# Three steps of an attention loop, each cut in two, with the second half at a later position

## The chip, the cores and the metric

The kernel runs on one core of a Trainium2 chip. A core has a matrix engine (PE in the profile, with its weight loads as PEld), a vector engine (DVE), a scalar engine (ACT), a general engine (POOL) and a queue engine that issues most transfers (SP). Each engine executes its own list of instructions in order, and waits for the others by semaphores. The metric is the device time of one launch in microseconds (us); of the kernel before, three runs are shown.

## The reference

One inference step of a trunk with two layers on 384 tokens (256 latent ones and 128 context ones, computed together, `NT` = 384). A layer is: half a SwiGLU feed-forward, a mixer, half a feed-forward, each behind an RMS norm whose scale, shift and gate come from a conditioning vector through a large weight (`w_ada`, 1024 x 9216). The mixer has three branches on one input projection:

```
q, k, v (6 heads, two key halves of 32)        differential attention, then
  o = rms_norm(o, subln_w) * (1 - lam_init)
cq -> rms_norm -> @ w_q_up (256 x 576)         6 heads of 96; the last 32 of each get rotary
ckv -> rms_norm -> keys and values             MLA softmax attention
u -> S5 scans -> y = gelu(y); y * sigmoid(y @ w_glu + b_glu)
out = concat(o_a, o_b, o_c) @ w_out
```

All of it is float32. The big products are made of three rounded products each (high by high, high by low, low by high).

## The kernel before, in words

Activations lie transposed (channels on the 128 partitions, tokens along the row). Most of the time goes to the two feed-forwards of each layer (`up`, `down`). The change is in the mixer's attention loop, which runs once in each layer, at about 425 to 575 us and 1250 to 1372 us of the profiled execution.

The loop has 36 units (`ORDER`): 18 of differential attention (`DA`, 'd') and 18 of MLA ('m'). A unit is one query tile `t` of one head or half: `scores` makes the products (`sc`; for DA four at once, each on 32 partitions), the maximum (`nm`, DVE), the exponential with its sum (`e`, ACT) and the scaling; three positions later (`LOOK`) `finish` transposes the weights (`wtp`) and, for the last tile, multiplies by the values (`po`). Other work is hung on the loop's positions by `put(i, step)`; what stands at position `i` is written `LEAD` = 2 units ahead of unit `i`. `AT` holds the positions of the steps that prepare MLA:

- `mla_q(t)`, for three token tiles: four products (`pq`), two copies on ACT into `qt2`, the rotation on DVE for the first two tiles, then six transposes (`qt2p`) and two copies into `qT2`. Its weight (`in_wsm`) takes one of the three `raw` buffers until the last tile is done.
- `norm_stats` and `norm_apply`, in the loop as `da_stats(b)` and `da_apply(b)`, for each of three head pairs once its `po` is done: squares on ACT (`nsq`), three small products (`npr<-co,nsq`), 13 tiny DVE instructions for the reciprocal root, six products that spread it (`npr<-co,tiny`), one DVE product, and the split for the output projection. Both steps stand at the same position.
- `s5_y` at the first position: gelu on ACT (`yg`), eight transposes (`ytp`), copies. `glu` follows at position 5.

Between them, `fill` issues pieces of the `w_ada` product for later layers: a load of 1 MB into a `raw` buffer (`in_wada`) and products `adaps`, four at once, each into 32 of the array's columns. All products write into a pool of seven PSUM banks. The order in which each engine gets its instructions isn't the order of the code: when the program is built, a scheduler plays it against a model of the engines and puts down at each time what is ready. So a change of one step moves the rows of others near it, and outside the loops nothing.

Of the kernel before, what the change touches and what calls it, by code (L numbers as in the profile page):

```python
# [9 lines left out]
F32 = mybir.dt.float32  # L10
FR = mybir.dt.float32r
I32 = mybir.dt.int32
AF = mybir.ActivationFunctionType
# [11 lines left out]
ORDER = 'd'*12+'dmm'*6+'m'*6  # L25
PF = (3, 8)
PFN = 1
LEAD, LOOK, QLEAD, DELAY, LAG, KCV = 2, 3, 4, 3, 0, 1
F0, F1 = 0, 36
AT = (0, 1, 2, 2, 3, 4, 4, 4, 5, 5, 7, 8, 8, 10, 11, 12, 13, 14)  # L30
AT5 = (0, 5)
YB = 8
KO = (6, 7, 0, 1, 2, 3, 4, 5)
# [143 lines left out]
def trunk(ctx, tc, I, O):  # L177
# [8 lines left out]
    def bank(name):  # L186
        return psp.tile([128, 512], F32, tag="P", name=name)
# [15 lines left out]
    hsum = co[:, CO['hsum'][0]:CO['hsum'][1]]  # L203
# [8 lines left out]
    def tt(out, a, b, op, eng=None):  # L212
        return (eng or V).tensor_tensor(out, a, b, op=op)  # L213

    def mul(out, a, b, eng=None):
        return tt(out, a, b, ALU.mult, eng)

    def add(out, a, b, eng=None):
        return tt(out, a, b, ALU.add, eng)
# [13 lines left out]
    def act(out, a, f, **k):  # L233
        S.activation(out, a, f, **k)  # L234
# [564 lines left out]
    def mixer(l, h, norm, P, s5stack, after, gate):  # L799
        oh, ol = [None], [None]  # L800
        with ExitStack() as ctx2:
            mp = ctx2.enter_context(tc.tile_pool(name="mix", bufs=1, reuse_waits="tile"))
# [30 lines left out]
            def scaled(ps, p=slice(0, 128), f=None):  # L833
                bb = mp.tile([128, 2], F32, tag="bb", name="bb", bufs=3)
                t = t384("pjt")
                if f is None:
                    V.tensor_copy(bb[p], ps[p, NT:NT + 2])
                    mul(t[p], ps[p, :NT], st['R'][p])
                else:
                    ts(bb[p], ps[p, NT:NT + 2], f)  # L840
                    stt(t[p], ps[p, :NT], f, st['R'][p], ALU.mult, ALU.mult)
                return t, bb

            def t384(name):
                return mp.tile([128, 384], F32, tag="t384", name=name, bufs=YB)
# [14 lines left out]
            def evac(ps):  # L860
                t, bb = scaled(ps)
                for c, lo_, hi_ in CR:
                    biased(t[:, lo_:hi_], t, bb, c)
                return t
# [25 lines left out]
            for z, ps in enumerate(p0):  # L890
                t, bb = scaled(ps)
                for c, lo_, hi_ in CR:
                    biased(uT[:, z, lo_:hi_], t, bb, c)
            vv = mp.tile([96, 8, 8, 16], F32, tag="vv", name="vv")
# [77 lines left out]
                    if nz is not None:  # L972
                        V.memset(fr[:, :, :, nz], 0.0)

            def norm_stats(tiles, sums, e=None):
                ps = [bank("npr") for _ in tiles]
                pm, c = ps[0][:, NT:512], 0
                for grp, sv in zip(tiles, sums):
                    n = sv.shape[-1]
                    sqs = []  # L980
                    for t in grp:
                        sqs.append(t384("nsq"))
                        act(sqs[-1], t, AF.Square)
                    for i in range(3):
                        for j, sq in enumerate(sqs):
                            T.matmul(pm[:, c + n * i:c + n * i + n], sq[:, 128 * i:128 * i + 128], sv,
                                     start=(j == 0), stop=(j == len(grp) - 1))
                    c += 3 * n
                return tiles, ps, rsqrt_small(pm[:, :c], c, e)
# [59 lines left out]
            v2, t = evac(p5[0]), evac(p5[1])  # L1049
# [23 lines left out]
            ap = ctx2.enter_context(tc.tile_pool(name="att", bufs=1, side="right", reuse_waits="tile"))  # L1073

            yT = mp.tile([128, 2, NT], F32, tag="t768", name="yT", bufs=4)

            def s5_y():
                yg = mp.tile([128, 8, 8, 16], F32, tag="vv", name="yg")
                for a in range(2):
                    act(yg.rearrange("p t g c -> p g t c")[:, 4 * a:4 * a + 4],  # L1080
                        py[a].rearrange("p (g t c) -> p g t c", g=4, t=8), AF.Gelu_apprx_tanh)
                for hf in range(2):
                    pt = bank("ytp")
                    for t in range(4):
                        T.transpose(pt[:, t * 128:(t + 1) * 128], yg[:, 4 * hf + t].rearrange("p g c -> p (g c)"),
                                    ident)
                    src = pt.rearrange("p (t g n) -> p g n t", t=4, g=2)[:, :, 0:48, :]
                    for g2 in range(2):
                        V.tensor_copy(yT[:, g2].rearrange("p (n t) -> p n t", t=8)[:, :, 4 * hf:4 * hf + 4], src[:, g2])
# [11 lines left out]
            def out_block(b, src):  # L1101
                act(oh[0][b][:, :NT], src, AF.Copy)
                sub(ol[0][b][:, :NT], src, oh[0][b][:, :NT])
# [36 lines left out]
            def rope(dst, src, nh, t):  # L1140
                a = t384("rsa").rearrange("p (h e) -> p h e", e=32)[:, 0:nh]
                b = t384("rsb").rearrange("p (h e) -> p h e", e=32)[:, 0:nh]
                mul(a, src, cosT[:, t, None, :].broadcast_to([128, nh, 32]))
                for x in range(2):
                    sv = src[:, :, 16 * x:16 * x + 16].rearrange("p n (h e) -> p n h e", h=2)
                    mul(b[:, :, 16 * x:16 * x + 16].rearrange("p n (h e) -> p n h e", h=2), sv[:, :, ::-1, :],
                        sinT[:, t, 16 * x:16 * x + 16].rearrange("p (h e) -> p h e", h=2)[:, None]
                        .broadcast_to([128, nh, 2, 8]))
                add(dst, a, b)
# [12 lines left out]
            su0 = [ap.tile([128, 6], F32, tag="su0", name="su0", bufs=3) for _ in range(3)]  # L1162
# [22 lines left out]
            oT = qT  # L1185
# [2 lines left out]
            ts(sw, SMV('subln')[:, l:l + 1], 1.0 - (0.8 - 0.6 * math.exp(-0.3 * l)))  # L1188
            dst = {}

            def da_stats(b):
                mul(su0[b], su0[b], su0[b])
                dst[b] = norm_stats([[oT[:, b]]], [hsum], su0[b])

            def da_apply(b):
                norm_apply(dst[b], [[sw]], [[[((0, NT), oT[:, b])]]])
                out_block(b, oT[:, b])
# [73 lines left out]

            wqb = []

            def mla_q(t):
                if not wqb:
                    wqb.append(load(I['wsm'][l, :, 0:1152], 1152)[:, :1152].rearrange("p (k n) -> p k n", k=2))
                wq = wqb[0]
                qt2 = ap.tile([128, 576], F32, tag="qt", name="qt2", bufs=2)
                for z in range(2):
                    pq = bank("pq")  # L1280
                    for k in range(2):
                        T.matmul(pq[:, 0:288], cT[:, k, t * 128:(t + 1) * 128], wq[:, k, 288 * z:288 * z + 288],
                                 start=(k == 0), stop=(k == 1))
                    act(qt2[:, 288 * z:288 * z + 288], pq[:, 0:288], AF.Copy)
                if t < 2:
                    pev = qt2.rearrange("p (h e) -> p h e", e=96)[:, :, 64:96]
                    rope(pev, pev, 6, t)
                for z in range(2):
                    pt = bank("qt2p")
                    for h_ in range(3):  # L1290
                        T.transpose(pt[:96, h_ * 128:(h_ + 1) * 128], qt2[:, (3 * z + h_) * 96:(3 * z + h_) * 96 + 96],
                                    ident)
                    act(qT2[:, 3 * z:3 * z + 3, t * 128:(t + 1) * 128],
                        pt[:96, :NT].rearrange("p (h n) -> p h n", h=3), AF.Copy, scale=MLA_SCALE)

            def mla_v(t):
                pt = bank("vt2p")
                T.matmul(pt[:, :384], ckT[:, t * 128:(t + 1) * 128], wv, start=True, stop=True)
                S.copy(vt2[:, t], pt[:, :384])
# [15 lines left out]
                units.append((da if c == 'd' else mla).pop(0))  # L1315
            KC = V.tensor_copy if KCV else S.copy
            pre = {}
            early = ([lambda t=t: mla_q(t) for t in range(3)] + [lambda t=t: mla_v(t) for t in range(4)])
            wraw = {}

            def wo(m, k0, k1, eng=None):
# [12 lines left out]
            def put(i, *fs):  # L1334
                pre.setdefault(i, []).extend(fs)

            def run(n, u, z, h):
                return lambda: late.__setitem__(n, part(u, z, h))

            prep = [lambda: None, lambda: None, lambda: cq_out(0), run('p6', 6, 1, 0), run('p6', 6, 1, 1),  # L1340
                    run('p7', 7, 0, 0), lambda: cq_out(1), lat_stats, run('p7', 7, 0, 1), kpe, lat_norm] + early
            for i, f in zip(AT, prep):
                put(i, f)
            put(AT5[0], s5_y)
            put(AT5[1], glu)
            for i, (kind, b, h2, t, wt) in enumerate(units):
                if t == 0 and h2 == 0 and kind == 'mla':
                    pre.setdefault(i, []).append(lambda b=b: mla_keys(b))
            for i, (kind, b, h2, t, wt) in enumerate(units):
                if kind == 'da' and h2 == 1 and t == 2:  # L1350
                    put(i + LOOK + LEAD + DELAY, lambda b=b: da_stats(b))
                    put(i + LOOK + LEAD + DELAY + LAG, lambda b=b: da_apply(b))
            for m in range(8):
                put(LEAD + W0 + W1 * m // 8, lambda m=m: wo(m, 0, NK1, G if WP else None))
            nfill = len(fillers)
# [1 line left out]
            for i in range(-LEAD, max(len(units) + LOOK, max(pre) - LEAD + 1)):  # L1357
                for f in pre.get(i + LEAD, []):
                    f()
                if 0 <= i < len(units):  # L1360
                    kind, b, h2, t, wt = units[i]
# [169 lines left out]
```

## Time and profile before

| | |
|---|---|
| runs shown | 1693.69 us (median of three), 1690.03 to 1694.74 |
| profiled execution | 1691.62 us, of which the span from first to last instruction is 1689.1 us |
| PE busy | 1638.3 us, 97% of the span |
| DVE, ACT, POOL busy | 65%, 41%, 9% |
| PE's share of the chain that ended last | 87% |
| granted clock of PE, mean | 0.992 of full speed |

PE is the engine that sets the time: the others wait for it. Its "busy" is an upper bound, since the end of a product is modelled. A list of PE in order of time gives the start of each run of like products, how long until the last is done, and in brackets the idle time before it and what ended it. Products overlap, so the cost of a run is best read from its start to the start of the next one. Each float32 product stands as two records in such a list (a transpose as one): "x8" of `sc` or `adaps` are four products.

### The profile page before, as it was taken

To read this page: it belongs to the slowest core of one execution; us is meant where nothing else is said; L and a number is where in the kernel's file an instruction comes from. 1 tells how busy PE (TensorE), PEld (TensorE's weight loads), DVE (VectorE), ACT (ScalarE), POOL (GpSimd) and SP (SyncE) were. 2 spreads that over 40 slices of the span, in tenths; PEclk is the share of its full clock that TensorE was granted. 3 is DMA by queue.
4 is the path that set the end of the run, shared out by engine and by line. 5 is a ranking of instruction groups with operands and counts; after the bars stand their busy time and mean duration, and the time that the engine had idled before them with its cause. 6 is when DMAs were issued, how large, how long until landed. Compare 5 with 4: busy or idle time off the path is not lost.

```text
span 1689.1 us, 26142 instructions
## 1 busy us (share of the span) xinstructions
PE 1638.3 (97%) x10144; PEld 1491.4 (88%) x10144; DVE 1099.7 (65%) x2752; ACT 690.1 (41%) x1295; POOL 157.5 (9%) x220
## 2 busy tenths in 40 slices
PE   7999999999999999999999999999998899999997
PEld 6888999998545889999999999999974589999997
DVE  5974577758456788577575555557655766555555
ACT  4332333433455543333343333334345654333333
POOL 1220010023001400000000000001311140000000
PEclk9999999999999999999999999999999999999998
DMA  9564543443477443353344333435337133333432
GB/s 376 194 222 154 146 148 105 145 175 117 154 275 276 159 140 135 125 137 120 100 152 173 119 126 112 143 94 172 133 113 251 51 116 114 124 121 118 138 97 84
DMA packets 45931, 251.47 MB, mean 149 GB/s; under 512 B 5600, under 2 KB 10576, under 8 KB 23920
## 3 DMA queue, kind: packets, MB, share of 16 engines
q1 hardware_dynamic: 41360, 241.12, 41.4%
q0 software_dynamic: 2144, 4.54, 1.1%
q10 hardware_dynamic: 2304, 4.15, 0.8%
q8 instruction: 79, 1.29, 0.3%
q14 instruction: 44, 0.36, 0.1%
HBM read 246.73 MB, written 3.05 MB: 148 GB/s over the span
## 4 chain that ended last, share of the span: by engine, by line
PE 87%; DVE 6%; ACT 3%; DMA 2%; issue 2%; POOL 0%; ACTq 0%; SPq 0%; DVEq 0%; POOLq 0%
PE up L239 15%; PE up L241 14%; PE up L240 14%; PE down L239 7%; PE down L241 7%; PE down L240 7%; PE adaps L293 4%; PE pj L239 2%; PE pj L241 2%; PE pj L240 2%; DMA raw<-in_wada 1%; PE pout L241 1%; PE pout L239 1%; PE pout L240 1%; PE po L1174 1%
## 5 line engine op out<-in xcount | busy, mean ns | idle before, releaser
L234 ACT ACTIVATE whi<-raw 128x1024 fp32r<-128x1024 f32 (+3 forms) x360 | 332.5, 926 | 658.8 <-PE up L240 333.5
L239 PE MATMUL up<-hh,whi 128*128 128x386 f32 x1408 | 474.4, 342 | 7.8 <-ACT whi L234 4.0
L241 PE MATMUL up<-hh,wlo 128*128 128x386 f32 x1408 | 478.5, 340 | 0.6 <-DVE wlo L213 0.6
L240 PE MATMUL up<-hl,whi 128*128 128x386 f32 x1408 | 478.5, 340 | 0.0
L213 DVE TENSOR_TENSOR wlo<-raw,whi 128x1024 fp32r<-128x1024 f32 (+2 forms) x318 | 347.7, 1093 | 49.3 <-ACT whi L234 46.5
L239 PEld LDWEIGHTS up<-hh,whi 128*128 128x128 f32 x1408 | 266.2, 190 | 15.6 <-ACT whi L234 5.3
L241 PEld LDWEIGHTS up<-hh,wlo 128*128 128x128 f32 x1408 | 265.7, 189 | 9.0 <-DVE wlo L213 2.2
L240 PEld LDWEIGHTS up<-hl,whi 128*128 128x128 f32 x1408 | 266.3, 189 | 1.6 <-issue 1.1
L241 PE MATMUL down<-hidh,wlo 128*128 128x384 f32 x704 | 236.3, 336 | 0.0
L239 PE MATMUL down<-hidh,whi 128*128 128x384 f32 x704 | 235.8, 335 | 0.0
L240 PE MATMUL down<-hidl,whi 128*128 128x384 f32 x704 | 235.3, 334 | 0.0
L231 DVE SCALAR_TENSOR_TENSOR xTt<-down,gate,xTt 128x256 f32<-128x256 f32 (+1 forms) x256 | 95.1, 414 | 114.9 <-PE down L241 114.9
L466 DVE COPY bb<-up 128x2 f32<-128x2 f32 x176 | 27.8, 159 | 190.0 <-PE up L241 189.5
L241 PEld LDWEIGHTS down<-hidh,wlo 128*128 128x128 f32 x704 | 132.1, 188 | 1.1 <-issue 0.6
L239 PEld LDWEIGHTS down<-hidh,whi 128*128 128x128 f32 x704 | 132.2, 188 | 1.0 <-ACT whi L234 0.8
L240 PEld LDWEIGHTS down<-hidl,whi 128*128 128x128 f32 x704 | 132.2, 188 | 0.0
L213 DVE TENSOR_TENSOR t<-up,R 128x384 f32<-128x384 f32 x176 | 95.5, 549 | 3.3 <-ACT R L234 3.2
L293 PE MATMUL adaps<-raw,conds 128*32 128x256 f32 (+1 forms) x704 | 84.7, 498 | 3.6 <-DMA raw<-in_wada 3.6
L239 PE MATMUL pj<-hh,whi 128*128 128x386 f32 (+1 forms) x240 | 83.2, 348 | 0.9 <-ACT whi L234 0.7
L234 ACT ACTIVATE hidh<-sl 128x384 fp32r<-128x384 f32 x88 | 46.1, 524 | 91.1 <-DVE sl L231 91.1
L241 PE MATMUL pj<-hh,wlo 128*128 128x386 f32 (+1 forms) x240 | 82.1, 343 | 1.2 <-DVE wlo L213 1.2
L240 PE MATMUL pj<-hl,whi 128*128 128x386 f32 (+1 forms) x240 | 81.5, 341 | 0.0
(268 smaller groups left out, 1953.0 us busy)
## 6 DMA issues: line engine op xcount, KB each, us to landing
raw<-in_wfi SPq DMA_DIRECT2D x85, 1024.0 KB, 4.9
raw<-in_wada SPq DMA_DIRECT2D x64, 1024.0 KB, 5.7
raw<-in_wfo SPq DMA_DIRECT2D x32, 768.0 KB, 4.2
raw<-in_wfo SPq DMA_DIRECT2D x32, 640.0 KB, 3.9
raw<-in_win SPq DMA_DIRECT2D x14, 1024.0 KB, 4.8
araw<-in_wada SPq DMA_DIRECT2D x8, 1024.0 KB, 9.8
raw<-in_wout SPq DMA_DIRECT2D x16, 512.0 KB, 3.5
wr<-in_wfi SPq DMA_DIRECT2D x8, 384.0 KB, 9.7
```

Source lines behind the costliest of these rows:

```text
L213: return (eng or V).tensor_tensor(out, a, b, op=op)
L231: return V.scalar_tensor_tensor(out, a, s, b, op0=op0, op1=op1)
L234: S.activation(out, a, f, **k)
L239: T.matmul(out, whi, xhi, start=first, stop=False)
L240: T.matmul(out, whi, xlo, start=False, stop=False)
L241: marks.append(T.matmul(out, wlo, xhi, start=False, stop=last).ins)
L293: T.matmul(ps[32 * q:32 * q + 32, 0:w], conds[:, k, :], raw[:, c0:c0 + w], start=(k == 0), stop=(k == 7))
L466: V.tensor_copy(bb[:, z], ps[z][:, NT:NT + 2])
L1174: T.matmul(po[64 * h2:64 * h2 + 64, 0:256], vt[:, kt, 128 * b + 64 * h2:128 * b + 64 * h2 + 64], wTs[h2][:, kt, :], start=(kt == 0), stop= ...
```

## The change

Each of the three steps is cut where PE has to wait for what ACT and DVE make of its products. `mla_q(t)` ends after the rotation, and the transposes are a step of their own, `mla_qt(t)`, two positions later (8 and 10, 9 and 11, 10 and 12; before, the first two tiles were at 8 and the third at 10). The tile `qt` gets a third buffer for it. The differential norm has its squares at position `i+6` of a head pair's last unit `i`, the sums and the root at `i+7`, the spreading at `i+9`; before, all of it was at `i+8`. The gelu stays at position 0, and its transposes come at 2. The instructions are the same in kind and number on each engine.

```diff
-LEAD, LOOK, QLEAD, DELAY, LAG, KCV = 2, 3, 4, 3, 0, 1
+LEAD, LOOK, QLEAD, KCV = 2, 3, 4, 1
-AT = (0, 1, 2, 2, 3, 4, 4, 4, 5, 5, 7, 8, 8, 10, 11, 12, 13, 14)
+AT = (0, 1, 2, 2, 3, 4, 4, 4, 5, 5, 7, 8, 10, 9, 11, 10, 12, 11, 12, 13, 14)
...
+            def norm_squares(tiles):
+                sqs = []
+                for grp in tiles:
+                    sqs.append([t384("nsq") for t in grp])
+                    for sq, t in zip(sqs[-1], grp):
+                        act(sq, t, AF.Square)
+                return sqs
...
-            def norm_stats(tiles, sums, e=None):
+            def norm_stats(tiles, sums, e=None, squares=None):
                 ps = [bank("npr") for _ in tiles]
                 pm, c = ps[0][:, NT:512], 0
-                for grp, sv in zip(tiles, sums):
+                for grp, sv, sqs in zip(tiles, sums, squares or norm_squares(tiles)):
                     n = sv.shape[-1]
-                    sqs = []
-                    for t in grp:
-                        sqs.append(t384("nsq"))
-                        act(sqs[-1], t, AF.Square)
...
-            def s5_y():
-                yg = mp.tile([128, 8, 8, 16], F32, tag="vv", name="yg")
+            yg = mp.tile([128, 8, 8, 16], F32, tag="vv", name="yg")
+
+            def s5_gelu():
                 for a in range(2):
                     act(yg.rearrange("p t g c -> p g t c")[:, 4 * a:4 * a + 4],
                         py[a].rearrange("p (g t c) -> p g t c", g=4, t=8), AF.Gelu_apprx_tanh)
+
+            def s5_y():
...
+            def da_squares(b):
+                mul(su0[b], su0[b], su0[b])
+                dst[b] = norm_squares([[oT[:, b]]])
+
             def da_stats(b):
-                mul(su0[b], su0[b], su0[b])
-                dst[b] = norm_stats([[oT[:, b]]], [hsum], su0[b])
+                dst[b] = norm_stats([[oT[:, b]]], [hsum], su0[b], dst[b])
...
-                qt2 = ap.tile([128, 576], F32, tag="qt", name="qt2", bufs=2)
+                qt2 = qts[t] = ap.tile([128, 576], F32, tag="qt", name="qt2", bufs=3)
...
                 if t < 2:
                     pev = qt2.rearrange("p (h e) -> p h e", e=96)[:, :, 64:96]
                     rope(pev, pev, 6, t)
+
+            def mla_qt(t):
+                qt2 = qts[t]
                 for z in range(2):
                     pt = bank("qt2p")
...
-            early = ([lambda t=t: mla_q(t) for t in range(3)] + [lambda t=t: mla_v(t) for t in range(4)])
+            early = [f for t in range(3) for f in (lambda t=t: mla_q(t), lambda t=t: mla_qt(t))]
+            early += [lambda t=t: mla_v(t) for t in range(4)]
...
-            put(AT5[0], s5_y)
+            put(AT5[0], s5_gelu)
+            put(AT5[0] + 2, s5_y)
...
-                    put(i + LOOK + LEAD + DELAY, lambda b=b: da_stats(b))
-                    put(i + LOOK + LEAD + DELAY + LAG, lambda b=b: da_apply(b))
+                    put(i + LOOK + LEAD + 1, lambda b=b: da_squares(b))
+                    put(i + LOOK + LEAD + 2, lambda b=b: da_stats(b))
+                    put(i + LOOK + LEAD + 4, lambda b=b: da_apply(b))
```

SP's list, which issues the loads, is the same row for row, and in each layer's loop POOL has one copy of a key moved by one place against a split. The lists of PE, ACT and DVE change within the two loops alone. Three places of PE's list in the second layer follow; the line numbers of the changed kernel are a little higher. `pq` and `qt2p` are the query projection and its transposes, `sc` scores, `adaps` the `w_ada` product, `wtp` transposed weights, `po` the product with the values, `npr` the norm, and `vt2p` MLA's values.

PE before, from the first query projection on:

```order
L1282 MATMUL pq<-raw,cT 128x288 x2
L293 MATMUL adaps<-raw,conds 32x512 x4
L1282 MATMUL pq<-raw,cT 128x288 x2
L293 MATMUL adaps<-raw,conds 32x512 x4
L1291 MATMUL qt2p<-co,qt_12963 96x128 x6
L1282 MATMUL pq<-raw,cT 128x288 x4
L293 MATMUL adaps<-raw,conds 32x512 x4
L1291 MATMUL qt2p<-co,qt_12988 96x128 x6
L1212 MATMUL sc<-kT,qT 128x384 x4
L1167 MATMUL wtp<-co,e 128x128 x3
L293 MATMUL adaps<-raw,conds 32x512 x4
```

PE now, from the same place:

```order
L1294 MATMUL pq<-raw,cT 128x288 x2
L1222 MATMUL sc<-kT,qT 128x384 x3
L1294 MATMUL pq<-raw,cT 128x288 x2
L1222 MATMUL sc<-kT,qT 128x384
L1174 MATMUL wtp<-co,e 128x128 x3
L293 MATMUL adaps<-raw,conds 32x512 x4
L1294 MATMUL pq<-raw,cT 128x288 x2
L293 MATMUL adaps<-raw,conds 32x512 x4
L1294 MATMUL pq<-raw,cT 128x288 x2
L1174 MATMUL wtp<-co,e 128x128
L1306 MATMUL qt2p<-co,qt_12963 96x128 x6
L1294 MATMUL pq<-raw,cT 128x288 x4
```

The transposes of the first tile stood behind its products and one run of `adaps`; now one score product, four transposed weights, two runs of `adaps` and the whole second tile's projection lie between. The four scores that stood together are three and one.

PE before, from the third tile on:

```order
L1167 MATMUL wtp<-co,e 128x128
L1282 MATMUL pq<-raw,cT 128x288 x4
L1291 MATMUL qt2p<-co,qt_13061 96x128 x6
L1212 MATMUL sc<-kT,qT 128x384 x4
L1167 MATMUL wtp<-co,e 128x128
L293 MATMUL adaps<-raw,conds 32x256 x8
L1174 MATMUL po<-wT,vtm 64x256 x6
L1177 MATMUL po<-wTp,vtm 64x128
L1298 MATMUL vt2p<-wsm,ckT 128x384
```

PE now, from the third tile's projection:

```order
L1294 MATMUL pq<-raw,cT 128x288 x4
L1222 MATMUL sc<-kT,qT 128x384
L293 MATMUL adaps<-raw,conds 32x512
L1222 MATMUL sc<-kT,qT 128x384
L293 MATMUL adaps<-raw,conds 32x512 x3
L1222 MATMUL sc<-kT,qT 128x384 x2
L1174 MATMUL wtp<-co,e 128x128
L1181 MATMUL po<-wT,vtm 64x256 x6
L1184 MATMUL po<-wTp,vtm 64x128
L1306 MATMUL qt2p<-co,qt_13007 96x128 x6
L1313 MATMUL vt2p<-wsm,ckT 128x384
```

The third tile's transposes, which came straight behind its products, aren't among these rows any more (they come after the next `adaps`); those of the second tile stand among them. The scores of one unit stand in three pieces, with one `adaps` product and then the other three between them.

PE before, around the first head pair's norm:

```order
L1237 MATMUL pk<-ckT,wsm 128x512
L293 MATMUL adaps<-raw,conds 32x256 x8
L986 MATMUL npr<-co,nsq 128x2 x3
L1167 MATMUL wtp<-co,e 128x128 x3
L1298 MATMUL vt2p<-wsm,ckT 128x384
L1212 MATMUL sc<-kT,qT 128x384 x4
L293 MATMUL adaps<-raw,conds 32x256 x8
L1167 MATMUL wtp<-co,e 128x128 x3
L1252 MATMUL sc<-kTh,qT_12625 128x384
L1167 MATMUL wtp<-co,e 128x128
L999 MATMUL npr<-co,tiny 64x128 x6
```

PE now, from the last `adaps` run ahead of that norm:

```order
L293 MATMUL adaps<-raw,conds 32x256 x5
L990 MATMUL npr<-co,nsq 128x2 x3
L1222 MATMUL sc<-kT,qT 128x128 x4
L1174 MATMUL wtp<-co,e 128x128 x3
L1313 MATMUL vt2p<-wsm,ckT 128x384
L293 MATMUL adaps<-raw,conds 32x256 x8
L1247 MATMUL pk<-ckT,wsm 128x512
L1174 MATMUL wtp<-co,e 128x128 x3
L1313 MATMUL vt2p<-wsm,ckT 128x384
L1222 MATMUL sc<-kT,qT 128x384 x3
L1003 MATMUL npr<-co,tiny 64x128 x6
L293 MATMUL adaps<-raw,conds 32x256 x3
```

The squares' sums (`npr<-co,nsq`) keep their place between `adaps` and `wtp`. A run of eight `adaps` products ahead of them is cut in three and five by `vt2p`, and the next unit's scores have moved in behind them.

## Rows read from the trace of the kernel before

**Rows 1.** The page: PE's busy time, and the issues of `in_wada` loads

```profile
PE 1638.3 (97%) x10144; PEld 1491.4 (88%) x10144; DVE 1099.7 (65%) x2752; ACT 690.1 (41%) x1295; POOL 157.5 (9%) x220
...
raw<-in_wada SPq DMA_DIRECT2D x64, 1024.0 KB, 5.7
```

**Rows 2.** PE's waits, whole span: engine, line, releaser, total us, times, longest us

```profile
PE adaps L293 <- DMA raw<-in_wada: 3.6, 4, 1.5
PE wtp L1167 <- ACT e L234: 3.3, 2, 1.8
...
PE qt2p L1291 <- DVE qt L213: 2.2, 3, 0.7
PE qt2p L1291 <- ACT qt L234: 2.1, 2, 1.8
PE sc L1212 <- ACT e L234: 1.5, 1, 1.5
PE npr L986 <- ACT nsq L234: 1.5, 1, 1.5
...
PE ytp L1085 <- ACT yg L234: 1.0, 2, 0.5
```

**Rows 3.** PE in order of time, second layer's loop: start, us, line, records, idle before

```profile
1264.69 0.91 PE L1212 MATMUL sc<-kT,qT 32*128 32x384 f32 x2
1265.53 1.27 PE L986 MATMUL npr<-lsum,nsq 128*128 128x1 f32 x10
...
1288.07 2.11 PE L1282 MATMUL pq<-raw,cT 128*128 128x288 f32 x8
1290.11 1.06 PE L293 MATMUL adaps<-raw,conds 128*32 128x512 f32 x8
...
1292.65 0.93 PE L1212 MATMUL sc<-kT,qT 32*128 32x384 f32 x8
1293.51 0.55 PE L1167 MATMUL wtp<-co,e 128*128 128x128 f32 x3
...
1295.15 2.38 PE L1282 MATMUL pq<-raw,cT 128*128 128x288 f32 x8
1299.31 0.86 PE L1291 MATMUL qt2p<-co,qt 128*96 128x128 f32 x6 [1.78 <-ACT qt L234]
```

**Rows 4.** PE in order of time, first layer's loop

```profile
444.23 3.04 PE L293 MATMUL adaps<-raw,conds 128*32 128x512 f32 x16
447.21 0.93 PE L999 MATMUL npr<-co,tiny 128*128 128x128 f32 x6
...
484.53 1.06 PE L293 MATMUL adaps<-raw,conds 128*32 128x256 f32 x12
485.51 0.48 PE L1212 MATMUL sc<-kT,qT 32*128 32x128 f32 x2
485.93 0.62 PE L293 MATMUL adaps<-raw,conds 128*32 128x256 f32 x2
486.48 0.55 PE L1167 MATMUL wtp<-co,e 128*128 128x128 f32 x3
...
493.61 1.92 PE L293 MATMUL adaps<-raw,conds 128*32 128x512 f32 x16
495.46 0.55 PE L1167 MATMUL wtp<-co,e 128*128 128x128 f32 x3
...
504.11 1.05 PE L293 MATMUL adaps<-raw,conds 128*32 128x512 f32 x2
505.09 0.43 PE L1177 MATMUL po<-wTp,vtm 128*64 128x128 f32 x2
```

**Rows 5.** Stretches: length, PE, PEld, DVE, ACT, POOL busy, granted clock, DMA, GB/s

```profile
440.00:450.00 10.00, 10.00 (x53) 5.13 (x52) 7.32 (x27) 2.14 (x6) 0.69 (x2) 0.83 0.33 122
450.00:460.00 10.00, 8.34 (x44) 4.03 (x42) 5.79 (x23) 8.32 (x21) 1.54 (x3) 0.84 0.62 234
1290.00:1300.00 10.00, 7.49 (x49) 3.55 (x48) 5.96 (x16) 6.43 (x19) 3.11 (x3) 1.00 0.41 138
1320.00:1330.00 10.00, 8.14 (x53) 4.58 (x51) 9.02 (x37) 6.51 (x22) 0.71 (x1) 1.00 0.01 2
```

More of the change, by code (lines that the diff above doesn't have):

```diff
@@ L1272, in mixer @@
             wqb = []
+            qts = {}
             def mla_q(t):
```

## The prediction

> **What bounds the kernel now.** First the page: PE is busy 1638.3 us, 97% of the span, DVE 65%, ACT 41% [rows 1]. So an edit is worth what it does to PE's list: the idle time it takes out or puts in, and the time of the products as they are cut and put together. Then PE's waits over the whole span [rows 2]: small everywhere, but the lines that the change touches are there. Last, PE in order of time within the two loops [rows 3, 4], read from the start of one run of products to the start of the next, since products overlap, and the 10-us stretches for the clock [rows 5]. Outside the two loops the order of every engine's instructions is unchanged, and nothing is taken for them.
>
> The sum is made against the profiled execution (1691.62 us), 2.07 us below the median of the runs shown (1693.69 us), a difference within their spread of 4.7 us. The result of the sum is added to the median.
>
> **The waits that go.** The waits for `qt` are 2.2 us (three times, DVE) and 2.1 us (twice, ACT) [rows 2]. Now the second tile's projection, `adaps` and transposed weights stand between: two runs of `adaps` alone are 1.85 us, one 0.93 us [rows 4], against a longest wait of 1.8 us. I take all 4.3 us as gone. The gelu's transposes come two positions later: 1.0 us. The norm's squares get a position of their own: 1.5 us [rows 2]; behind the squares `adaps` products now stand ahead of their sums.
>
> A wait also costs a little more than its bracket. From the third tile's projection to its transposes there are 4.16 us, where the same eight records take 2.04 us when other products follow, so the wait whose bracket says 1.78 us cost 2.12 us [rows 3]: the pipeline empties and fills, 0.34 us. That is the largest; for nine waits I take 0.15 us each, 1.3 us.
>
> The wait of `adaps` for its load (3.6 us, four times, longest 1.5 us [rows 2]) goes in part, though no load is moved. The query weight holds one of three `raw` buffers until the last `pq`. Before, `adaps` of the next buffer came 1.5 us behind it, and the load from issue to landing takes 5.7 us [rows 1]; now about 5.7 us of scores, `adaps` and `po` lie between by the list and the durations above. I take 2.0 us; the bounds are 0 (the loads elsewhere are late as before) and 3.6 us.
>
> The scores' wait of 1.5 us for an exponential and one of the two waits of `wtp` (3.3 us together, longest 1.8 us [rows 2]) stand at the loop's head, behind the exponentials of the gate and what ACT does for it; that part isn't moved, and I leave them, 3.0 us. The other, 1.8 us, is where DVE is busy 9.02 us of 10 and PE 8.14 [rows 5]; the moved norm loosens it, and I take 1.2 us of it (bounds 0 and 1.8). Waits together: 4.3 + 1.0 + 1.5 + 1.3 + 2.0 + 1.2 = 11.3 us less.
>
> **The work that is added.** The instructions are the same in number, but not how they stand. Four scores on 32 partitions each, or four `adaps` products on 32 columns each, run beside each other when they are neighbours. A score product by itself takes 0.84 us (1264.69 to 1265.53), four in a row 0.86 us (1292.65 to 1293.51) [rows 3]. An `adaps` product of 512 by itself takes 0.98 us, a quartet 0.93 us (1.85 us for two); one of 256 by itself 0.55 us, six 0.98 us [rows 4]. So a quartet that is cut in two costs a whole quartet more. PE's list, counted piece by piece over both loops:
>
> Scores of 384 columns: 7 pieces in each layer before, 11 now, 8 more in all; 8 x 0.84 = 6.7 us. The third tile's place shows one such: four in a row before, and 1, 1 and 2 with `adaps` between now. Scores of 128 columns in the first layer: two pieces fewer, at 0.42 us each (485.51 to 485.93 [rows 4]), 0.8 us less. `adaps` of 512: three pieces more (one cut into 1 and 3 stands at the same place), 3 x 0.98 = 2.9 us. `adaps` of 256: in the second layer four runs of eight before, now 8, 8, 5, 3, 3, 3, 1, 1, which at 0.55 us for one and at 1.0 us for eight (near the six of rows 4) is 1.8 us more; in the first layer 0.9 us less; 0.9 us more in all. Together 6.7 - 0.8 + 2.9 + 0.9 = 9.7 us more. The upper bound is this sum. The lower is 0: where PE would have stood at a cut anyway, the cut is free. I take the whole, as PE is busy 97% and the scores that are cut stand between products that don't wait [rows 3].
>
> **What stays or isn't in the trace.** The second steps issue no transfer, and SP's list is row for row the same, so no load moves past another by order. POOL exchanges two neighbours in each layer, taken as 0, since it is idle for nine tenths of the span [rows 1]; without that cover a score waits, 1.5 us by the nearest row [rows 2]. DVE and ACT get the same instructions in another order; ACT has the split of a weight ahead of a copy of `qt2` at one place, at most 0.5 us, hidden by what now stands before the transposes. A new price is that the norm's bank is held from the sums at `i+7` to the spreading at `i+9`, so that one of seven banks is missing for two positions, six times. No row of before shows a product that waits for a bank there. Below it is 0; above, I use the nearest row, a score that waited 1.5 us [rows 2], twice, 3.0 us. I take 0, nearest to [rows 3], where scores follow at once. New waits of `adaps` for loads where its runs stand closer: 0 to 1.5 us, the longest in [rows 2]; taken 0.
>
> **Sum.** -11.3 + 9.7 = -1.6 us: the profiled execution would take 1690.0 us, and the median 1693.69 - 1.6 = 1692.1 us. With each term at its ends, the unknown ones apart, this case reaches from about 1688.5 to 1696.
>
> **Clock.** In the stretches from 440 to 460 us the granted clock is 0.83 and 0.84, a mean of time at 2.4 and at 1.2 GHz, though PE is busy 10.00 and 8.34 us; in 1290 to 1300 us, with the 1.78 us wait in it and PE busy 7.49 us, it stays at 1.00 [rows 3, 5]. Two `adaps` quartets at 444.23 took 2.98 us, where two take 1.85 us at the full clock [rows 4]. The stretch loses 0.17 x 10 + 0.16 x 10 = 3.3 us, and in the sum it stays where it is. The Trainium skill, "TensorE: Matmul & The Clock Gate", Part 1, says that the gate follows how busy the engine has been recently; by that rule fewer waits keep the clock up. These two rows speak against so plain a reading: the stretch with the least busy PE is the one at full rate.
>
> **Rivals.** *The cuts cost little.* The order puts a score between other products because the banks or DVE's maxima come free one at a time; then a quartet in one piece would have waited, and a cut fills that time. For it: between 1320 and 1330 us DVE is busy 9.02 us and PE 8.14 [rows 5]. Against: the four scores at 1292.65 went at once [rows 3]. With a third of the added work, 3.2 us, the sum is -11.3 + 3.2 = -8.1, 1685.6 us. The Trainium skill, "Trainium Kernel Development and Optimization", Best Practices, says that packing products into parts of the array speeds up the products and not the emptying of PSUM, which is this rival's reason in general; the DVE row agrees in one stretch of the loop and no row shows it for the rest.
>
> *The clock stays up.* The order around 440 to 460 us changes, and the loss of 3.3 us goes: -1.6 - 3.3 = -4.9, 1688.8 us. For it: the products there are other neighbours now. Against: what brings the clock down is there with PE busy all the time [rows 5].
>
> *Slower: the cut scores make the softmax late.* A unit's last scores now come up to 0.84 + 0.98 + 0.84 + 0.98 = 3.6 us after its first (third tile, with the durations above), the maximum and exponential follow it, and the transposed weights stand where they stood. If that uses up the cushion of three positions, `wtp` waits at each cut unit about what the cut costs, 8 x 0.84 = 6.7 us: -1.6 + 6.7 = +5.1, 1698.8 us. It decides once the delay is longer than the work between scores and transposes. For it: `wtp` has the second largest wait, 3.3 us [rows 2], so the cushion fails already at two places. Against: both of these stand behind something else, as said.
>
> *It doesn't do what it says:* the transposes still wait for `qt`. PE's list has them far behind their projection, so hardly.
>
> **How the numbers follow.** This kernel's measurement can tell about 0.3%, 5.1 us, from no change. The forecast 0.49, nine tenths of it within 5.1 us and the rest below; the cheap cuts 0.22, faster; the clock 0.13, on the border and half faster; the late softmax 0.14, on the border to slower, and most of its chance beyond it since a late `wtp` also delays what follows; not as said 0.02, no change. That gives faster 0.22 + 0.07 + 0.05 = 0.34, slower 0.14, no change 0.52. The range reaches from the cheap cuts to the late softmax, 1685 to 1699; the forecast's own is 1688.5 to 1696.
>
> **What would show it.** Right: no waits of PE for `qt`, `yg` or `nsq` among the longest; scores and `adaps` in more pieces, a score by itself still about 0.84 us; PE busy about as long as before. The cheap cuts would show as a busy time of PE that falls or stays while its waits fall by 11 us; the clock as a rate of 1.00 between 440 and 460 us; the late softmax as waits of `wtp` for `e` well above 3.3 us; the norm's bank as products that wait for DVE's reading of `npr`. I am wrong in the main step if PE's list shows cut scores that take much less than 0.84 us from their start to the next.

## The result: 0.4 to 0.6% slower

The changed kernel takes 1701.97 us (median of four runs, 1700.72 to 1702.79), the kernel before beside it 1692.24 us (four runs): a ratio of 1.0056, interval 1.0039 to 1.0074. Six later runs gave 1699.27 us and 1.0041 (1.0026 to 1.0055). The forecast was 1692.1 us, its range ended at 1699: it is wrong, and on the other side from where its sum pointed.

The page of the changed kernel, its profiled execution with a span of 1700.1 us:

```profile
PE 1652.4 (97%) x10144; PEld 1496.2 (88%) x10144; DVE 1096.3 (64%) x2752; ACT 688.5 (40%) x1295; POOL 157.3 (9%) x220
```

PE's share is as before [rows 1], with 14.1 us more busy. PE's waits over the whole span in the changed kernel, longest sums first where they differ from those of before (columns as in [rows 2]):

```profile
PE adapt L301 <- ACT ad L234: 4.7, 3, 3.5
...
PE npr L990 <- ACT nsq L234: 2.9, 4, 1.2
PE pj L241 <- DVE wlo L213: 2.8, 4, 0.8
PE wtp L1174 <- ACT e L234: 2.6, 2, 1.5
...
PE npr L1003 <- DVE tiny L231: 1.5, 1, 1.5
PE sc L1222 <- ACT e L234: 1.5, 1, 1.5
...
PE sc L1262 <- DVE nm L1164: 1.4, 1, 1.4
...
PE adaps L293 <- DMA raw<-in_wada: 0.5, 1, 0.5
```

The waits that the change aimed at are gone: no row for `qt` or `yg` is left, and `adaps` waits 0.5 us for its loads, 3.6 before [rows 2]. But `npr` for the root (`tiny`) and `sc` for a maximum (`nm`) have rows that weren't there, and the waits for `ad`, `nsq` and `wlo` are longer. The rows above add up to 17.9 us; those of before that they answer to, with those that are gone, to 20.6 us ([rows 2] and four that stood outside it: `py` 2.8, `pj` 1.2, `sc` 0.9, `adapt` 0.5). So 2.7 us of waits went, where 11.3 were expected.

The second layer's loop of the changed kernel, PE in order of time, at the places of [rows 3]:

```profile
1293.21 1.24 PE L1294 MATMUL pq<-raw,cT 128*128 128x288 f32 x4
1294.28 0.27 PE L1174 MATMUL wtp<-co,e 128*128 128x128 f32 x1
1294.39 0.82 PE L1306 MATMUL qt2p<-co,qt 128*96 128x128 f32 x6
1295.04 2.11 PE L1294 MATMUL pq<-raw,cT 128*128 128x288 f32 x8
1297.08 0.91 PE L1222 MATMUL sc<-kT,qT 32*128 32x384 f32 x2
1297.92 1.04 PE L293 MATMUL adaps<-raw,conds 128*32 128x512 f32 x2
1298.89 0.91 PE L1222 MATMUL sc<-kT,qT 32*128 32x384 f32 x2
```

Behind the second tile's `pq` the first tile's transposes follow at 1294.39 without a wait. A score by itself still takes 0.84 us (1297.08 to 1297.92) and a lone `adaps` of 512 0.97 us: the prices of the cuts were right.

Clock and work come apart in the runs' own figures. Each run has a mean granted clock; the time multiplied by it is an estimate of what the launch would take at full rate, and the rest of what half rate costs. Means over the runs, in us (the medians and ratios beside them):

| kernel | median (runs) | ratio to before, interval | granted clock | time x clock | rest |
|---|---|---|---|---|---|
| before, beside e1 to e4 | 1691.9 (29) | | 0.9929 | 1679.8 | 12.0 |
| before, beside e5 to e8 | 1692.6 (19) | | 0.9927 | 1679.6 | 12.3 |
| before, beside e9 to e12 | 1691.6 (35) | | 0.9929 | 1679.5 | 11.9 |
| changed | 1702.0 (4) | 1.0056, 1.0039 to 1.0074 | 0.9902 | 1685.3 | 16.6 |
| e5: changed, again | 1699.3 (6) | 1.0041, 1.0026 to 1.0055 | 0.9920 | 1685.5 | 13.6 |
| e1: gelu alone | 1705.1 (4) | 1.0084, 1.0071 to 1.0097 | 0.9900 | 1688.2 | 17.1 |
| e2: query and norm | 1694.1 (12) | 1.0017, 1.0005 to 1.0030 | 0.9935 | 1683.1 | 11.0 |
| e3: query alone | 1689.8 (11) | 0.9990, 0.9981 to 0.9999 | 0.9941 | 1680.2 | 10.0 |
| e4: norm alone | 1697.1 (12) | 1.0030, 1.0015 to 1.0044 | 0.9921 | 1683.5 | 13.4 |
| e6: e1, `ad` by DVE | 1703.4 (6) | 1.0070, 1.0049 to 1.0091 | 0.9905 | 1688.2 | 16.2 |
| e7: gelu, first layer | 1698.4 (9) | 1.0037, 1.0023 to 1.0050 | 0.9919 | 1684.5 | 13.8 |
| e8: e1, projection later | 1692.6 (12) | 1.0001, 0.9988 to 1.0014 | 0.9924 | 1679.7 | 12.8 |
| e9: squares alone | 1695.6 (12) | 1.0019, 1.0008 to 1.0030 | 0.9928 | 1682.7 | 12.1 |
| e10: changed, projection later | 1694.3 (12) | 1.0015, 1.0003 to 1.0028 | 0.9926 | 1681.8 | 12.6 |
| e11: query, and gelu as in e8 | 1689.1 (12) | 0.9989, 0.9977 to 1.0000 | 0.9958 | 1682.3 | 7.2 |
| e12: all, mended | 1688.5 (12) | 0.9985, 0.9972 to 0.9997 | 0.9943 | 1679.0 | 9.6 |

Of the changed kernel's loss some 6 us are work and waits, and 1 to 5 us clock, by this split. It gives the clock too much: over the 83 runs of the kernel before, 0.001 more clock goes with 1.1 us less time, where the product takes 1.7 us.

### The profile page after: what moved, and what is told of

Its sections match the earlier page's. It is cut to its first block, busy times and chain, and to the rows that moved or that the text cites. A ratio compares the mean times of both kernels' runs of the same rounds, so it can differ in the third digit from the quotient of the medians.

```text
span 1700.1 us, 26137 instructions
## 1 busy us (share of the span) xinstructions
PE 1652.4 (97%) x10144; PEld 1496.2 (88%) x10144; DVE 1096.3 (64%) x2752; ACT 688.5 (40%) x1295; POOL 157.3 (9%) x220
## 4 chain that ended last, share of the span: by engine, by line
PE 88%; DVE 7%; ACT 3%; issue 2%; DMA 1%; POOL 0%; SPq 0%; DVEq 0%; ACTq 0%
PE up L239 14%; PE up L241 14%; PE up L240 14%; PE down L241 7%; PE down L239 7%; PE down L240 7%; PE adaps L293 4%; PE pj L239 2%; PE pj L241 2%; PE pj L240 2%; PE pout L239 1%; PE pout L241 1%; PE pout L240 1%; PE wtp L1174 1%; PE po L1181 1%
```

## The experiments

**Which of the three steps (e1 to e4).** Each of these takes the changed kernel and puts some steps back where they were (e1 and e4 also have two buffers of `qt` again). With all three put back, the lists of PE, ACT and DVE are those of the kernel before, row for row.

```diff
 # the query step back (e1, e4)
-AT = (0, 1, 2, 2, 3, 4, 4, 4, 5, 5, 7, 8, 10, 9, 11, 10, 12, 11, 12, 13, 14)
+AT = (0, 1, 2, 2, 3, 4, 4, 4, 5, 5, 7, 8, 8, 8, 8, 10, 10, 11, 12, 13, 14)
 # the norm back (e1, e3): squares, sums and spreading all at
+                    put(i + LOOK + LEAD + 3, ...)
 # the gelu's transposes back (e2, e3, e4)
-            put(AT5[0] + 2, s5_y)
+            put(AT5[0], s5_y)
```

Gelu alone (e1):

> Only the gelu and its transposes are in two steps; MLA's query step and the norm are as before. Theory N (a new wait): the changed kernel's first loop has PE stand 3.5 us at the transposes of ad, since ACT's copy of ad now stands behind a table load and three exponentials, and the clock falls to half rate behind it. This comes from the gelu's step alone, so this kernel takes 3 to 5 us more than before (about 1696 us on before's 1692), with the wait of 3.5 us in its trace. Rival C (cut scores): the loss comes from scores and w_ada products standing in more pieces, which the query step and the norm cause; then this kernel is within 1 us of before.

Query and norm, without the gelu (e2):

> The query step and the norm are in steps, the gelu is as before. Theory N with the half-clock stretch of the second loop (1337 to 1351 us in the changed kernel) as the other part: the wait for ad is gone (-3.5 to -5 us against the changed kernel), the stretch stays, about +5 us against before. Rival C (cut scores): as slow as the changed kernel, +9 to +10 us against before.

Query alone (e3):

> Only MLA's query step is in two. Theory H (the long half-clock stretch of the second loop comes from the moved norm, whose sums and spreading stand before it): -2 us against before, since the waits for qt go (4 us) and some scores are cut (2 us), and the granted clock of the second loop is as before. Rival C (cut scores): +4 to +6 us, with PE's waits for qt gone and no more half clock than before.

Norm alone (e4):

> Only the norm is in three steps at its new positions. Theory H (the norm brings the long half-clock stretch): +5 to +7 us against before, with a granted clock well under 0.9 over the 40 us before the last head pair is done. Rival C (cut scores by the query step): within 1.5 us of before, granted clock as before.

Measured against before: gelu +13.2 us, query -2.1, norm +5.2, query and norm +2.2. The query step is the size that theory H gave, but not by its sum: time x clock is as before (1680.2 and 1679.8), so that the waits that go are paid by the cuts, and the 2 us are in the clock. Rival C falls for the query step, since e3 has cut scores and is no slower. The gelu is most of the loss, as theory N has it, but at 13 us, not 3 to 5; and e2, which N put at +5, is at +2.2. The norm is the second part, in H's size, but only 1.4 us of it is clock (13.4 and 12.0), so that H's reason falls. The three don't add up (+16.3 apart, +7 to +10 together).

Why the gelu's transposes matter is seen where they stand. PE before, at the head of the first layer's loop (`py` is S5's output, `pj` the late half of the input projection, and many rows of `pj` between are left out):

```profile
426.82 0.64 PE L293 MATMUL adaps<-raw,conds 128*32 128x256 f32 x8
427.96 1.09 PE L1085 MATMUL ytp<-co,yg 128*128 128x128 f32 x8 [0.51 <-ACT yg L234]
428.81 0.42 PE L239 MATMUL pj<-hh,whi 128*128 128x386 f32 x1
...
430.85 0.34 PE L241 MATMUL pj<-hh,wlo 128*128 128x386 f32 x1
431.11 0.93 PE L1212 MATMUL sc<-kT,qT 32*128 32x384 f32 x8
431.97 0.44 PE L239 MATMUL pj<-hh,whi 128*128 128x386 f32 x1
...
434.02 0.34 PE L241 MATMUL pj<-hh,wlo 128*128 128x386 f32 x1
434.20 0.38 PE L301 MATMUL adapt<-co,ad 128*128 128x128 f32 x2
```

PE now, at the same place:

```profile
428.95 0.34 PE L241 MATMUL pj<-hh,wlo 128*128 128x386 f32 x1
429.22 0.64 PE L293 MATMUL adaps<-raw,conds 128*32 128x256 f32 x8
429.79 1.09 PE L1092 MATMUL ytp<-co,yg 128*128 128x128 f32 x8
430.81 0.93 PE L1222 MATMUL sc<-kT,qT 32*128 32x384 f32 x8
431.67 0.63 PE L293 MATMUL adaps<-raw,conds 128*32 128x256 f32 x6
435.81 0.52 PE L301 MATMUL adapt<-co,ad 128*128 128x128 f32 x2 [3.51 <-ACT ad L234]
436.01 0.65 PE L239 MATMUL pj<-hh,whi 128*96 128x386 f32 x1
436.45 0.53 PE L240 MATMUL pj<-hl,whi 128*96 128x386 f32 x1
```

Before, `adaps` and the transposes come first, then `pj` products, the first scores at 431.11, and `pj` products again up to 434.20: the second lot covers the maximum and exponential of the first scores. The step `s5_y` now stands at position 2 behind the first half of that projection. PE takes the `pj` products ahead of `adaps` and of the transposes; that removes a wait of 0.51 us. The scores come at 430.81, 0.3 us earlier than before. Beside their exponentials PE has `adaps` alone; then it stands 3.51 us for the copy `ad`, and resumes at half rate (the `pj` product at 436.45 takes 0.53 us, the one at 430.85 of before 0.34). PE takes its list in order: twelve `pj` products stand behind `adapt`, and run without a wait once it is done.

ACT before and now, at the same place:

```profile
427.81 0.38 ACT L234 ACTIVATE ad<-adaps 128x256 f32<-128x256 f32 x1
432.69 1.28 ACT L234 ACT_TABLE_LOAD   x1 [4.51 <-DVE nm L1157]
```

```profile
432.39 1.28 ACT L234 ACT_TABLE_LOAD   x1 [5.99 <-DVE nm L1164]
433.69 0.58 ACT L234 ACTIVATE e<-sc,nm 128x384 f32<-128x384 f32 x1
...
434.26 0.57 ACT L234 ACTIVATE e<-sc,nm 128x384 f32<-128x384 f32 x1
...
434.81 0.58 ACT L234 ACTIVATE e<-sc,nm 128x384 f32<-128x384 f32 x1
...
435.37 0.39 ACT L234 ACTIVATE ad<-adaps 128x256 f32<-128x256 f32 x1
```

The copy `ad` is now behind the table load and three exponentials; before, it was ahead of them. The products that it copies are done at 432.30 (431.67 and 0.63 us), before the table load begins, so that it is ACT's order which holds it up for 3 us.

**Is it ACT's queue (e6)?** The one copy `ad` is made by DVE (the third of the kernel; `adn`, not shown, counts them). Five of PE's 10144 records differ from e1's in kind, all behind the wait, at 442 to 446 us.

```diff
-                act(ad[:, :w], ps[:, :w], AF.Copy)
+                (act(ad[:, :w], ps[:, :w], AF.Copy) if len(adn) != 2
+                 else V.tensor_copy(ad[:, :w], ps[:, :w]))
```

> As the kernel with the gelu alone in two steps, but the one copy of ad that stood behind the exponentials is made by DVE. Theory N (PE's 3.5 us wait there is ACT's queue, and costs what it shows): 3 to 5 us less than that kernel, about 1701 us. Rival W (the wait moves: PE stands as long at the next product, since what hid the first exponentials has been used up): within 1 us of it.

1703.4 us, 1.6 us under e1, and the intervals overlap: not the 3 to 5 us of theory N. PE and DVE in that run:

```profile
431.90 0.63 PE L294 MATMUL adaps<-raw,conds 128*32 128x256 f32 x6
436.19 0.44 PE L303 MATMUL adapt<-co,ad 128*128 128x128 f32 x2 [3.65 <-DVE ad L298]
```

```profile
435.18 0.16 DVE L1231 RECIPROCAL rsu<-su 128x1 f32<-128x1 f32 x1 [1.71 <-ACT e L234]
435.26 0.54 DVE L1166 TENSOR_REDUCE nm<-sc 128x1 f32<-128x384 f32 x1
435.72 0.41 DVE L298 COPY ad<-adaps 128x256 f32<-128x256 f32 x1
```

The wait is as long (3.65 us) with another engine at its end: DVE takes `ad` at 435.72, behind a reciprocal that waited 1.71 us for an exponential. Both engines' queues lead through the first exponentials. The edit didn't take the wait away, so it doesn't decide between the two theories: N's price for the wait isn't tested by it, and W's next product was never reached. What it shows is that another engine is no cure where its queue passes the same exponentials. A copy ahead of them wasn't run.

**One layer (e7), and the projection (e8).** In e7 the gelu is split in the first layer only; in e8 the split stays, and the first half of the projection goes one position later, so that it is behind the transposes again. PE's records in e8 differ from before's in kind at 46 of 10144 places, ACT's at none.

```diff
 # e7, to e1
+            put(AT5[0] + (2 if l == 0 else 0), s5_y)
 # e8, to e1
-AT = (0, 1, 2, 2, 3, 4, ...
+AT = (0, 1, 2, 3, 3, 4, ...
```

> The gelu in two steps in the first layer only. Theory S (each layer's loop pays for itself, as the profile of the kernel with both says: 5 to 7 us in each loop): 5 to 8 us more than before. Rival C2 (most of the loss is the clock and the cut pieces of the second loop): 0 to 2.5 us more than before; and rival N2 (the wait for ad, which only the first loop has, is nearly all): 11 us or more.

> The gelu's transposes stay two positions later, but the first half of the late projection is put one position later too, so that it stands behind the transposes again. Theory P (the loss comes from the projection's products being spent ahead of the transposes, where they no longer cover the first exponentials): within 2 us of before. Rival G (the later transposes themselves cost, since what reads them comes later): 8 us or more above before.

e7 is 5.8 us slower than before by the medians, so each layer has about half (theory S). In e1 the second layer has no wait for `ad` to show: there the loss is in cut products (see "Waits and work apart"). e8 is at 1.0001: theory P holds as to what has to be moved, the projection's products. It doesn't tell the lost cover from `ad`'s place in ACT's queue, since it puts both back. PE in e8:

```profile
427.03 1.09 PE L1092 MATMUL ytp<-co,yg 128*128 128x128 f32 x8 [0.51 <-ACT yg L234]
428.06 0.93 PE L1222 MATMUL sc<-kT,qT 32*128 32x384 f32 x8
428.91 0.45 PE L239 MATMUL pj<-hh,whi 128*128 128x386 f32 x1
...
433.09 0.34 PE L241 MATMUL pj<-hh,wlo 128*128 128x386 f32 x1
433.26 0.38 PE L301 MATMUL adapt<-co,ad 128*128 128x128 f32 x2
```

The `pj` products stand behind the scores, all of them, and `adapt` follows at 433.26 without a wait. The wait of 0.51 us for `yg` is back: the split itself gained nothing that wasn't paid for by the projection's products.

**The long stretch at half rate (e5).** The changed kernel again.

> The changed kernel itself, profiled and timed a second time. Theory O (the long half-clock stretch of the second loop belongs to the order of the products): the stretch from 1337 to 1351 us is there again, and the time is 1701 to 1703 us. Rival L (it falls by chance in one execution and not in another): the stretch is shorter by half or elsewhere, and the runs spread by 5 us or more.

Its first profile has a stretch of half rate in the second loop that the kernel before doesn't have; the second profile has little of it. The two, 1330 to 1350 us, columns as in [rows 5]:

```profile
1330.00:1340.00 10.00, 7.57 (x39) 4.48 (x36) 7.41 (x22) 6.25 (x21) 0.61 (x1) 0.84 0.00 0
1340.00:1350.00 10.00, 10.00 (x41) 6.20 (x40) 5.33 (x22) 4.14 (x13) 0.61 (x1) 0.50 0.01 2
```

```profile
1330.00:1340.00 10.00, 7.56 (x42) 4.15 (x35) 7.78 (x25) 6.42 (x21) 0.61 (x1) 0.84 0.00 1
1340.00:1350.00 10.00, 10.00 (x60) 6.88 (x59) 6.98 (x29) 6.33 (x20) 1.88 (x2) 0.94 0.01 2
```

The lists are the same, and one execution has a granted clock of 0.50 for ten microseconds, with PE busy all the time, the other 0.94. Its span is 1694.5 us against 1700.1. Both fall to half rate between 1330 and 1340 us (0.84), and only the first stays there. Theory O falls: the length of the stretch is one execution's, not the order's. Rival L holds for the stretch; the six runs spread by 3.7 us, where it said 5 or more. What stays in every run is the 5.7 us of work and waits (table).

**The norm (e9) and the mended kernels (e10 to e12).** In the lists the sums (`npr<-co,nsq`) stand one unit nearer behind the `po` that their squares need: the change has them at `i+7`, where they were at `i+8`. With nothing but the spreading one position later, the lists are those of before row for row, so that its later place alone does nothing. The place of the norm shown ahead of the prediction is the first pair's, which has no wait before or now. PE in the changed kernel, for the other two pairs of the second layer:

```profile
1323.93 0.43 PE L1184 MATMUL po<-wTp,vtm 128*64 128x128 f32 x2
1325.57 0.83 PE L990 MATMUL npr<-co,nsq 128*128 128x2 f32 x6 [1.21 <-ACT nsq L234]
...
1361.18 0.43 PE L1184 MATMUL po<-wTp,vtm 128*64 128x128 f32 x2
1362.81 0.83 PE L990 MATMUL npr<-co,nsq 128*128 128x2 f32 x6 [1.20 <-ACT nsq L234]
```

The waits are 1.21 and 1.20 us, before one of 1.5 us; the whole span has 2.9 us for `nsq`, before 1.5 [rows 2].

```diff
 # e9 (norm alone, to e4) and e12
-                    put(i + LOOK + LEAD + 2, lambda b=b: da_stats(b))
+                    put(i + LOOK + LEAD + 3, lambda b=b: da_stats(b))
 # e9 besides
-                    put(i + LOOK + LEAD + 4, lambda b=b: da_apply(b))
+                    put(i + LOOK + LEAD + 3, lambda b=b: da_apply(b))
 # e10 (to the changed kernel), e11 (with the norm back) and e12
-AT = (0, 1, 2, 2, 3, 4, ...
+AT = (0, 1, 2, 3, 3, 4, ...
```

> Only the norm is changed: its squares come two positions earlier than in the kernel before, its sums and its spreading stay at the old position. Theory Q (the norm's loss of 5 us comes from the sums, which the change puts one position nearer to the product that they need, so that PE's waits for nsq stay or grow): within 1.5 us of before, with no wait for nsq above 0.5 us. Rival A (ACT's earlier squares delay the exponentials behind them): 4 us or more above before, with PE's waits for e or wtp up.

> The changed kernel with the first half of the late projection one position later, behind the gelu's transposes. Theory P (the projection spent ahead of the transposes is the loss, in the changed kernel too): 5 to 8 us less than the changed kernel, 1 to 3 us above before, and no wait for ad of more than 1 us. Rival I (the three steps disturb each other, and the gelu's part is small beside the other two): 2 us less than the changed kernel or nothing, 5 us or more above before.

> The query step in two and the gelu in two with the late projection behind the transposes; the norm as before. Theory M (each wait removed without a spent cover is a gain): 2 to 4 us less than before, the query step's 2 us and up to 1 us for the gelu. Rival Z (a wait taken away here comes back at the next): within 1 us of before.

> All three steps cut, with the late projection behind the gelu's transposes, and with the norm's sums and spreading at their old position, the squares alone earlier. Theories P and Q together: 2 to 5 us less than before. Rival R2 (the norm's squares cost by themselves): 1 us or more above before.

e12's spreading stayed at its new place, `i+9`, not at the old one. e10 is 5 to 8 us faster than the changed kernel, and 2.7 us above before, as theory P has it. e9 is 4.0 us slower than before, where theory Q said at most 1.5: Q doesn't hold there, with a wait of 1.0 us for `nsq` left; the exponentials' waits that rival A names are no larger than before either (1.5 us for `e` in the first loop). With the query step cut, Q's time does hold: e12 and e10 differ by the place of the sums alone, and the ratios are 0.9985 (to 0.9997) and 1.0015 (from 1.0003). e12 has the lowest median, 3.1 us below before, with an interval that ends just under 1; e11 (-2.5 us) is the lower end of theory M and can't be told from e12. By the split of the table, e11's gain is in the clock, not in the work, and so is most of e12's.

**Waits and work apart.** PE's list in order of time says where each kernel pays. For each loop, from the first `py` to the first `up` behind it, "idle" is the sum of the waits in brackets, and "work" is the length of the loop without them and without what half rate took, (1 - granted clock) x time. Each row is one execution; the two of the changed kernel agree within 0.8 us in each figure, and the sums come out up to 2 us above those by time x clock. In us, first loop + second loop:

| kernel | idle | work | both, against before |
|---|---|---|---|
| before | 6.8 + 12.5 | 165.6 + 138.4 | |
| changed | 9.2 + 7.1 | 168.7 + 144.3 | +6.0 |
| e5: changed, again | 10.0 + 7.1 | 168.5 + 144.9 | +7.2 |
| e1: gelu alone | 12.6 + 10.5 | 166.7 + 143.9 | +10.4 |
| e8: e1, projection later | 7.5 + 13.3 | 165.9 + 137.2 | +0.6 |
| e3: query alone | 3.7 + 7.3 | 171.6 + 142.9 | +2.2 |
| e9: squares alone | 6.2 + 10.2 | 168.3 + 142.8 | +4.2 |
| e10: changed, projection later | 5.6 + 7.5 | 168.5 + 145.5 | +3.8 |
| e12: all, mended | 6.0 + 7.5 | 167.9 + 142.6 | +0.7 |

The gelu pays by waits in the first loop (5.8 us more idle) and by cut products in the second: there it has 5.5 us more work and less idle time, `adaps` of 256 stand in 10 pieces where they were 6, and scores of 128 columns in 8 where they were 5; e8 has 6 and 5 again. e9 waits 2.9 us less than before and works 7.1 us more, all of it in `adaps` and `sc`: its loss is in cut pieces too. And e12 waits as long as e10 (13.5 and 13.1 us) and works 3.5 us less, so that the reason of theory Q, the waits for `nsq`, isn't what tells them apart, though these did fall (2.9 us in e10, 1.0 in e12). Why a moved step cuts its neighbours in one place and not in another is the scheduler's, and wasn't looked into.

## Why the prediction was wrong, point by point

**The gelu's term has the wrong sign.** "The gelu's transposes come two positions later: 1.0 us", a gain, was the step that failed first. By itself the step costs 13.2 us (e1), and nothing once the projection is moved with it (e8). The working looked at the wait of `ytp` and not at what the step is moved past: position 2 holds the first half of the projection, half of whose products stood beside the first exponentials. The places chosen for reading the order were those of the query and norm; the loop's head wasn't among them, and "ACT get the same instructions in another order" passed over the one that mattered, `ad` behind three exponentials.

**The norm's term as well.** "The norm's squares get a position of their own: 1.5 us" counted a wait as gone whose sums the change puts nearer to their source. The waits for `nsq` grew to 2.9 us; the norm alone costs 5.2 us.

**The other waits were right.** `qt` 4.3 us: gone. `adaps` for its loads: 3.1 us less, 2.0 taken, within the bounds. The waits at the loop's head stayed (`wtp` 1.5, `sc` 1.5). What went with `qt` was paid back in cuts (e3).

**New waits stood at 0.** The prediction named three (a bank, a load, a copy of `qt2`) and took each as 0; others came. The profile shows 4.2 us more for `ad`, 1.5 us for the root (`npr<-tiny`), 1.4 us for a maximum, 1.6 us more for `wlo`: 8.7 us. With the waits for `nsq` they are why -11.3 became -2.7; a wait of 2.8 us for `py`, which no term named, went as well.

**The added work was about right.** 9.7 us were forecast. Time at full clock went up by 5.7 us, with 2.7 us less waiting: 8.4 us for the cuts, by these two figures (the one a mean of runs, the other one execution's). The rows of both loops give 9.0 us directly, with 6.6 us for scores of 384 columns, where the forecast had 6.7. The cheap-cuts rival falls with it.

**The rivals.** The slower one ended on the right side with the wrong mechanism: `wtp` waits less than before (2.6 us for 3.3), so cut scores don't make the softmax late. The clock between 440 and 460 us did rise to 1.00 in the changed kernel's profile, as that rival has it, but fell elsewhere; over the runs the change loses 1.3 to 4.6 us to it (13.6 and 16.6 against 12.3 and 12.0). The rule weighed there (the Trainium skill, "TensorE: Matmul & The Clock Gate", Part 1: the gate follows how busy the engine has been) agrees with the stretch from 436 us, which follows a wait of 3.51 us; it doesn't with the ten microseconds of half rate at PE busy 10.00, which the same list had in one execution and hardly in the next.

## What to carry to other kernels

Before a step is moved to a later position, list what it is moved past on the engine that sets the time: independent work that it lets ahead is spent there, and the other engines' copies move with it (here 13.2 us; whether the lost cover or ACT's order makes the wait of the first loop isn't decided). When a step is cut to separate producer and consumer, look at the consumer's distance before and after: a cut can also bring it nearer. A wait removed from the list is a gain only when neither the other waits nor the work of products that get cut grow by as much: the changed kernel and e9 wait 3 us less than before in all, and are slower.

## What the runs showed of the hardware

One program's time varies with the clock more than most edits here move it. The twelve runs of e4 span 1692.5 to 1703.2 us, and the mean granted clock of these two is 0.995 and 0.989: 0.006 of 1700 us is 10 us, the spread of these two. Over many runs the clock is worth less: 1.1 us for 0.001 in the 83 runs of the kernel before. For differences below 0.5%, a kernel's single profile says little about its time unless the stretches at half rate are taken out of both.
